# The first norm's rows kept feature set by feature set, for the experts' gather

## The chip, the cores and the metric

The program runs on one core of one Trainium2 chip. The metric is the device time of one execution in microseconds (us). A core has TensorE (PE, with its weight loads shown apart as PEld), VectorE (DVE), ScalarE (ACT), GpSimd (POOL) and SyncE (SP), whose queue issues the large transfers. All memory below is the on-chip memory of 128 partitions, unless HBM is named.

## The reference

Two layers over 256 tokens of 1024 features. A layer is a token mixer (three attention branches, gated, then an output projection), a norm, a mixture of experts, and a second norm. Cut to what matters here:

```python
for l in range(DEPTH):                                   # DEPTH = 2
    mix = token_mixer(x, ...)                            # ends with merged @ w_o
    x = layer_norm(alpha * x + mix, ln1_g[l], ln1_b[l])  # the first norm
    ffn = hier_moe(x, w_group, b_group, w_sub, b_sub, w1, w3, w2)
    x = layer_norm(alpha * x + ffn, ln2_g[l], ln2_b[l])

def hier_moe(t, ...):          # each token: the best of 4 groups, 2 of its 8 experts
    for e in range(N_EXPERTS):                           # 32 experts, hidden width 256
        h = jax.nn.silu(t @ w1[e]) * (t @ w3[e])
        y = y + combine[:, e:e + 1] * (h @ w2[e])
```

## The kernel before

**Tokens and experts.** The 256 tokens are two tiles of 128 (`t` = 0, 1), with tokens on partitions. An expert has 32 slots for tokens. Experts are worked on in quads of four, so a quad has 128 slots. The router finds a token's place in its experts; `dispatch` writes a 0/1 matrix "tokens by slots" from it.

**The gather.** For each of eight sets of 128 features, `gather_k` multiplies the transposed normed rows with the 0/1 matrix, so that a quad's 128 slots stand with features on partitions (`xg`). The stationary operand is `self.xn[:, t, k + i]`, 128 tokens by 128 features, and the moving operand is 128 slots of the 0/1 matrix. A product of f32 operands is two pairs of weight load and matmul. A quad takes 8 sets x 2 token tiles x 2 = 32 pairs; a layer has 8 quads. ScalarE then applies the norm's gain and bias out of PSUM (L1654). The first quad is gathered before the experts start; of each later quad, 16 pairs run ahead of the second product of the quad before and 16 behind it.

**Which features make a set.** Set k is the features f = 8q + k with q = 0..127, because a partition of the experts' weights holds eight consecutive features. `self.xn` is therefore a view of the row tile:

```python
self.xn = self.x.rearrange("p t (q k) -> p t k q", k=KD)   # KD = 8, set once per layer
```

A stationary tile of this view takes every eighth f32 of a row, 32 bytes apart. `ln1_xn` (steps `X0`, `X1`) writes the norm without gain and bias over `x` itself, in order. `ln1_out` reads `x` in order for the residual rows (with gain and bias, 512 features at a time) that start the second norm's sums.

**What sets the order.** Each engine runs its instructions in the order of the program text. From the output projection to the first experts that order is the list `END`: `... X0 X1 E s00 ... s16 N e0 e1 rk G3 pl pm d0 d1 cb g2 ct wt g0 g4 g6 st si`. `X` is the norm, `E` loads the table for the exponentials, `e` are the router's exponentials, `cb` its weights (DVE), `wt` the weighted 0/1 matrix (POOL, L1641), `g` gathers, and `st` transposes the weighted matrix (TensorE, L1663). Then `moe` goes from quad to quad: w1 product and w3 product (L1691), gather of half of the next quad, transposes (L1737), second product (L1771, behind the other half of the gather from the second quad on), and sums over slots (L1757) one quad later.

**Weights and slots.** All large tiles, temporaries and weights, share 24 slots of 8 KiB a partition (`Slots`). `Ring` issues the weights on SP's queue in order of use, each as soon as a dry pass over the program says that a slot can be spared until its use. A layer's experts have some 100 MB of weights, in transfers of 1 MB for most of them; the last quad's w3 and w2 come in pieces of 256 and 512 KB (L193).

Of the kernel before, what the change touches and what calls it, by code (L numbers as in the profile page):

```python
# [10 lines left out]
F32 = mybir.dt.float32  # L11
# [33 lines left out]
# Columns of the output projection, and of the last experts' second product: the last ones are few, as a norm waits for them.  # L45
# [5 lines left out]
# Splits of weights run so many pieces ahead of their products.  # L51
# [4 lines left out]
# The steps of the last layer's end.  # L56
# [5 lines left out]
# The piece by which a queue of attention steps is to be through, and the tensor work left for what lies between two steps.  # L62
# [53 lines left out]
class Slots:  # L116
    """8 KiB slots that the weight stream and the large temporaries share."""
# [23 lines left out]
    def part(self, name, n):  # L141
        """One of n parts of a slot."""
        for p in self.shared[n]:
            if p["free"]:
                return Part(self, n, p, p["free"].pop())
        p = {"tile": self.alloc([P, n, 2048 // n], F32, name), "free": set(range(1, n))}
        self.shared[n].append(p)
        return Part(self, n, p, 0)
# [17 lines left out]
class Ring:  # L166
    """Weights in the order of their use, each loaded as soon as a slot can be spared until then.

    `plan` is what a dry pass over the program has found: the slots that its temporaries hold after
    each change, and the change at which each weight tile is released."""  # L170
# [43 lines left out]
class Dry:  # L214
    """Stands for every object of the language in the dry pass."""
# [13 lines left out]
class Trunk:  # L229
# [35 lines left out]
    def evac(self, out, in_, n):  # L265
        """PSUM to SBUF on the engine of the two that has less to do."""
        if self.busy["act"] + 200 + 0.83 * n < self.busy["dve"] + 70 + 1.04 * n:
            self.note("act", n)
            self.nc.scalar.activation(out, in_, AF.Copy)
        else:  # L270
            self.note("dve", n)
            self.nc.vector.tensor_copy(out, in_)  # L272

    def split(self, hi, lo, src, n):
        """src = hi + lo exactly, each of 12 significant bits."""
        self.note("act", n)
        self.note("pool" if self.lo_pool else "dve", n)
        self.nc.scalar.activation(hi, src, AF.Copy)  # L278
        (self.nc.gpsimd if self.lo_pool else self.nc.vector).tensor_tensor(lo, src, hi.bitcast(F32), op=ALU.subtract)  # L279
# [7 lines left out]
    def warm(self, n, src):  # L287
        """Products that nobody reads: the tensor engine's clock falls to half when it has little to do."""
        ps = self.bank()
        for _ in range(n):  # L290
            self.nc.tensor.matmul(ps, src[:, 0:P], src[:, 0:512], start=True, stop=True)

# [105 lines left out]
    def load_small(self, l, home, o):  # L398
        """The layer's vectors, off the weights' queue; the router's weights behind the first o floats of a slot."""
# [19 lines left out]
    def small_T(self):  # L419
        """The vectors with their features on partitions; the router's weights with the gain of its input taken in."""  # L420
        nc = self.nc
        ps = self.bank()
        nc.tensor.transpose(ps[:, 0:P], self.v, self.ident)
        self.vec = self.t([P, 59], F32, "vecT", 1)
        nc.vector.tensor_copy(self.vec, ps[:, 0:59])
        self.hbg = self.t([P, 24], F32, "hbg", 1)
        nc.vector.tensor_scalar(self.hbg, self.vec[:, 3:27], 0.5, None, op0=ALU.mult)
        self.wg = self.t([P, KD, 36], F32, "wg", 1)
        w = self.wgb[:, :, 36:72]
        for j in range(2):  # L430
            g = self.vec[:, 27 + 8 * j:35 + 8 * j, None].broadcast_to([P, KD, 36])
            nc.gpsimd.tensor_tensor(self.wgb[:, :, 36 * j:36 * j + 36], w, g, op=ALU.mult)
        nc.gpsimd.tensor_copy(self.wg, self.wgb[:, :, 0:36])

    def small_rows(self):
        """Sums over the features: what a token's mean and the input's bias add to its logits."""
# [15 lines left out]
    def spread_gains(self, gb):  # L452
        """The first partition's rows to all."""
# [8 lines left out]
    def step(self, f, need=None, cost=0.45, key=None, after=()):  # L462
        """An attention step: what it needs marked, its tensor time, and steps that must lie some tensor time back."""
        self.q["steps"].append((f, need, cost, key, after))
# [17 lines left out]
    def run_fg(self, budget):  # L482
        """Attention steps worth so much tensor time, the most urgent first."""
# [7 lines left out]
    def run_fg_until(self, mark):  # L491
        """Everything of a branch that is left, other branches' steps where it would wait."""
# [6 lines left out]
    def rate(self, i):  # L499
        """Tensor time of attention steps that a piece must be joined by for all to be done when due."""  # L500
# [29 lines left out]
    def pieces(self, l):  # L530
        """The mixer's dense products in order: each is (key of its weights, last use, prepare, product)."""
# [67 lines left out]
        def gates(br, q):  # L599
            """Two 128-column tiles of a branch's gate."""  # L600
# [26 lines left out]
        def outp(br, w, kt, i, need):  # L627
            """A branch's output columns, gated and summed: 256 or 512 columns at a time."""
# [108 lines left out]
    def rope(self, v, t, nh, half, c, s):  # L737
        """Rotates the leading dims of [128, heads, dims] in place."""
# [13 lines left out]
    # -- branch A --  # L752
# [73 lines left out]
    # -- attention units: (block 0, four heads) or (block 1, two heads), 512 scores a row --  # L826
    def scores(self, us):
        """Score products, mask, maximum, exponentials of a unit, or of two on different rows of the array."""
# [38 lines left out]
    def probT(self, us):  # L867
        """Transposes of the 512 probability columns of one unit, or of two that share them."""
# [14 lines left out]
    def pv(self, ps, us, first, last):  # L883
        """Adds the outputs of two units, even heads and odd heads, each pair of heads in 128 columns."""
# [27 lines left out]
    def units_pipe(self, mk, oT, done, free, needs, first, joint):  # L912
        """Scores of a pair of units, then their transposes and outputs."""
# [63 lines left out]
    # -- branch C --  # L977
# [136 lines left out]
    # -- branch B --  # L1114
# [15 lines left out]
    def b_merge(self):  # L1130
        """Weights of the groups from their maxima and sums."""
# [167 lines left out]
    def mixer(self, l, acts):  # L1299
# [33 lines left out]
        self.xn = self.x.rearrange("p t (q k) -> p t k q", k=KD)  # L1333
# [19 lines left out]
    def table(self, func):  # L1353
        """Has the function's table loaded before it is waited for."""
# [3 lines left out]
    # -- first layer norm of a token tile, and the router's logits; x becomes twice alpha * x + the mixer's output  # L1358
    # (the products carry the gates' factor 2) --
# [30 lines left out]
    def grow(self):  # L1390
        """A slot more for the experts: half of it the rows of four, the rest two tiles of 512."""
# [7 lines left out]
    def ln1_rs(self, t):  # L1399
        """Mean, 1 / deviation, and the product's negative."""  # L1400
# [28 lines left out]
    def ln1_xn(self, t):  # L1429
        """The norm but for its gain and bias, in place."""  # L1430
        nc = self.nc
        mv = self.ln1[t][1]
        nmr = self.t([P, 1], F32, "nmr", 2)
        nc.gpsimd.tensor_tensor(nmr, mv[:, 3:4], mv[:, 2:3], op=ALU.mult)
        nc.scalar.activation(self.x[:, t], self.x[:, t], AF.Identity, bias=nmr, scale=mv[:, 2:3])

    def spread_row(self, j):
        """512 features of the first norm's gain (and then its bias), on all partitions."""
# [6 lines left out]
    def ln1_out(self, t, h):  # L1445
        """Half of a token tile's norm itself."""
        x = self.take()
        hs = slice(h * 512, (h + 1) * 512)
        g, b = self.gain1[h], self.gain1[2 + h]
        v = self.nc.vector  # L1450
        v.tensor_tensor(x, self.x[:, t, hs], g, op=ALU.mult)
# [3 lines left out]
    def residual(self, xs, h):  # L1455
        """Starts the token tiles' sums with their rows."""
# [4 lines left out]
    # -- second layer norm of a token tile --  # L1461
# [9 lines left out]
    def ln2_rs1(self, t):  # L1471
        """Mean, deviation, -1/2 of its square, of the sums that the chip holds over ALPHA."""
# [6 lines left out]
    def ln2_rs2(self, t):  # L1479
        """1 / deviation, and its product with the mean's negative."""  # L1480
# [17 lines left out]
    def next_T(self, t):  # L1498
        """The next layer's input, features on partitions."""
# [9 lines left out]
    def next_y(self, t, h):  # L1509
        """Half of it: gain and bias are a feature's own there."""  # L1510
# [17 lines left out]
    def ln2_out(self, t, acc, c, pool):  # L1528
        """A quarter of a token tile's rows of the last layer's output."""
# [13 lines left out]
    def route(self, l):  # L1543
        """The router, step by step: each token's best group, the first two of its experts, their weights, and its
        place among an expert's tokens. What a match replaces is the first of its value: among the first eight, a
        group, as the groups come before the experts."""
# [70 lines left out]
    def rows_of(self, e):  # L1617
        """The rows in the slots of four experts."""
        return self.xgs[e // Q % 2][:, 0:1024].rearrange("p (k c) -> p k c", k=KD)

    def dispatch(self, e0):
        """Tokens by slots of experts e0..e0+7."""
# [21 lines left out]
    def gather_k(self, pm, j, xg, k):  # L1644
        """Two times 128 features of the rows in the slots of four experts, gain and bias added."""
# [10 lines left out]
    def slots_T(self, e):  # L1656
        """Slots by tokens: the combine matrix of four experts and the weights of its slots."""
# [15 lines left out]
    def moe(self, l):  # L1673
# [9 lines left out]
        for e in range(0, NE, Q):  # L1683
# [111 lines left out]
            if e == NE - 2 * Q:  # L1795
                self.slots.free(self.x)
# [50 lines left out]
    def overflow(self, l, acc):  # L1847
        """Adds the outputs of the tokens past an expert's capacity."""
# [101 lines left out]
```

## Time and profile before

| | before |
|---|---|
| median of 3 runs, us | 1023.01 (1022.1 to 1024.78) |
| span of the profiled execution, us | 1022.9 |
| PE / PEld busy, us | 955.5 / 770.8 |
| DVE / ACT / POOL busy, us | 473.9 / 416.6 / 161.7 |
| read from HBM | 282.44 MB |
| mean granted clock of TensorE | 0.970 |

The profile is of one execution. The three runs are the device times of others. PE's busy time is a union over pipelined instructions, so it is not PE at its peak. The experts of the first layer run from some 300 to 505 us of the span, those of the second from some 808 to 1011 us.

### The profile page before, as it was taken

Reading aid. Unit: us, or ns where it says so; the run is one execution under the profiler, and the core shown is the slowest. Engines: PE = TensorE matmul, PEld = TensorE weight load, DVE = VectorE, ACT = ScalarE, POOL = GpSimd, SP = SyncE. Lnnn points to the kernel's source line nnn. Section 1 sums busy time; section 2 is a strip of 40 time slices with the busy share of each in tenths; the row PEclk is TensorE's granted clock in tenths of the full one; section 3 lists DMA queues with packets and bytes.
Section 4 is the critical chain, followed back from the end, with each engine's and each line's share of the span. In section 5 each row is a group of like instructions: output and inputs, shape, how many; then the busy total and the mean of one; then the engine's idle time right before and its main releaser. Section 6 shows DMA issues by size and latency. Waiting matters only on the chain.

```text
span 1022.9 us, 18674 instructions
## 1 busy us (share of the span) xinstructions
PE 955.5 (93%) x7584; PEld 770.8 (75%) x7591; DVE 473.9 (46%) x968; ACT 416.6 (41%) x911; POOL 161.7 (16%) x274
## 2 busy tenths in 40 slices
PE   8999999999999997879879999999999999977794
PEld 7888899899986774556469888998999867654462
DVE  5747776845642110111398586676455420101014
ACT  5545646644442221112345646665354422211131
POOL 4531210021100110000156071000311000000001
PEclk9999999999999998889989999999999999989898
DMA  9933261696969999999992134426968799999993
GB/s 330 328 103 124 79 210 42 220 340 216 365 241 380 417 400 419 418 417 375 376 340 68 64 124 128 162 90 224 330 232 321 288 379 420 419 419 417 419 370 121
DMA packets 100170, 284.76 MB, mean 278 GB/s; under 512 B 6324, under 2 KB 53808, under 8 KB 78576
## 3 DMA queue, kind: packets, MB, share of 16 engines
q1 hardware_dynamic: 99088, 283.12, 73.7%
q8 instruction: 62, 1.02, 0.4%
q0 software_dynamic: 992, 0.39, 0.2%
q14 instruction: 28, 0.23, 0.1%
HBM read 282.44 MB, written 1.05 MB: 277 GB/s over the span
## 4 chain that ended last, share of the span: by engine, by line
PE 68%; DMA 17%; issue 7%; POOL 3%; DVE 3%; SPq 1%; ACT 1%; POOLq 0%; DVEq 0%; ACTq 0%
DMA w<-in_w_dram 15%; PE bank L283 12%; PE bank L284 12%; PE bank L285 12%; PE bank L1650 7%; PE bank L1691 7%; PE bank L837 3%; PE bank L1771 3%; DMA w<-in_w_in_dram 2%; PE bank L891 2%; PE bank L878 2%; PE bank L1757 1%; PE bank L840 1%; PE bank L1459 1%; DVE xTl L279 1%
## 5 line engine op out<-in xcount | busy, mean ns | idle before, releaser
L279 DVE TENSOR_TENSOR ws<-w,ws 128x1024 fp32r<-128x1024 f32 (+2 forms) x154 | 184.7, 1208 | 133.1 <-ACT ws L278 124.2
L278 ACT ACTIVATE ws<-w 128x1024 fp32r<-128x1024 f32 (+2 forms) x158 | 159.0, 1023 | 35.5 <-PE bank L285 15.9
L1691 PE MATMUL bank<-w,xg 128*32 128x256 f32 x2048 | 139.6, 413 | 33.9 <-DMA w<-in_w_dram 24.4
L1691 PEld LDWEIGHTS bank<-w,xg 128*32 128x32 f32 x2048 | 70.2, 118 | 105.1 <-DMA w<-in_w_dram 30.5
L1650 PEld LDWEIGHTS bank<-xg,x 128*128 128x128 f32 x512 | 124.2, 334 | 3.0 <-issue 2.5
L1650 PE MATMUL bank<-xg,x 128*128 128x128 f32 x512 | 125.7, 399 | 0.0
L283 PE MATMUL bank<-ws,xTh 128*128 128x408 f32 (+3 forms) x320 | 116.6, 364 | 1.2 <-ACT xTh L278 1.2
L1654 ACT ACTIVATE xg<-bank,gpk 128x128 f32<-128x128 f32 x128 | 51.7, 454 | 159.3 <-PE bank L1650 159.3
L283 PE MATMUL bank<-xTh,ws 128*128 128x256 f32 x384 | 111.2, 290 | 0.0
L285 PE MATMUL bank<-ws,xTl 128*128 128x408 f32 (+3 forms) x320 | 110.6, 346 | 0.6 <-DVE xTl L279 0.6
L284 PE MATMUL bank<-ws,xTh 128*128 128x408 f32 (+3 forms) x320 | 110.3, 345 | 0.0
L284 PE MATMUL bank<-xTl,ws 128*128 128x256 f32 x384 | 108.6, 283 | 0.0
L285 PE MATMUL bank<-xTh,ws 128*128 128x256 f32 x384 | 108.5, 283 | 0.0
L1721 DVE SCALAR_TENSOR_TENSOR t<-t,cw,bank 128x256 f32<-128x256 f32 x16 | 10.8, 677 | 157.2 <-PE bank L1691 157.2
L283 PEld LDWEIGHTS bank<-xTh,ws 128*128 128x128 f32 x384 | 73.5, 191 | 1.8 <-issue 1.0
L284 PEld LDWEIGHTS bank<-xTl,ws 128*128 128x128 f32 x384 | 73.6, 192 | 0.2
L285 PEld LDWEIGHTS bank<-xTh,ws 128*128 128x128 f32 x384 | 73.5, 191 | 0.0
L283 PEld LDWEIGHTS bank<-ws,xTh 128*128 128x128 f32 x320 | 61.4, 192 | 8.1 <-ACT xTh L278 1.8
L853 ACT ACTIVATE p<-bank,nb 128x128 f32<-128x128 f32 (+1 forms) x92 | 37.3, 420 | 69.9 <-DVE nb L845 65.1
L285 PEld LDWEIGHTS bank<-ws,xTl 128*128 128x128 f32 x320 | 61.0, 191 | 5.9 <-DVE xTl L279 1.6
L284 PEld LDWEIGHTS bank<-ws,xTh 128*128 128x128 f32 x320 | 61.3, 192 | 3.4 <-DVE ws L279 0.3
L1771 PE MATMUL bank<-w,t 128*32 128x512 f32 (+1 forms) x544 | 59.1, 571 | 1.0 <-DVE t L272 1.0
(361 smaller groups left out, 1530.2 us busy)
## 6 DMA issues: line engine op xcount, KB each, us to landing
w<-in_w_dram SPq DMA_DIRECT2D x168, 1024.0 KB, 15.7
w<-in_w_gate_dram SPq DMA_DIRECT2D x24, 1024.0 KB, 5.3
w<-in_w_dram SPq DMA_DIRECT2D x80, 256.0 KB, 7.2
w<-in_w_in_dram SPq DMA_DIRECT2D x18, 1024.0 KB, 7.7
w<-in_w_in_dram SPq DMA_DIRECT2D x12, 816.0 KB, 12.8
w<-in_w_o_dram SPq DMA_DIRECT2D x8, 1024.0 KB, 8.8
w<-in_w_a_dram SPq DMA_DIRECT2D x4, 1024.0 KB, 6.1
w<-in_w_c_dram SPq DMA_DIRECT2D x4, 1024.0 KB, 5.1
```

The lines of the kernel that those rows point to most:

```text
L278: self.nc.scalar.activation(hi, src, AF.Copy)
L279: (self.nc.gpsimd if self.lo_pool else self.nc.vector).tensor_tensor(lo, src, hi.bitcast(F32), op=ALU.subtract)
L283: m(out, sh, mh, start=start, stop=False)
L284: m(out, sh, ml, start=False, stop=False)
L285: m(out, sl, mh, start=False, stop=stop)
L837: nc.tensor.matmul(b[:, j * w:(j + 1) * w], q[:, blk * P:(blk + 1) * P], k[:, 0:w], start=j == 0, stop=False)
L853: nc.scalar.activation(p[:, j], v[:, j], AF.Exp, bias=nb[:, j:j + 1], scale=u["scale"], accum_out=sm[:, j:j + 1])
L878: nc.tensor.transpose(ps[:, n * P:(n + 1) * P], p[:, j * P:(j + 1) * P], self.ident)
L1650: nc.tensor.matmul(ps[:, i * P:(i + 1) * P], self.xn[:, t, k + i], pm[:, t, j:j + Q].rearrange("p e c -> p (e c)"), start=t == 0, stop=t = ...
L1654: nc.scalar.activation(xg[:, k + i], ps[:, i * P:(i + 1) * P], AF.Identity, bias=b, scale=g)
L1691: nc.tensor.matmul(hp[i * CAP:(i + 1) * CAP, c * 256:(c + 1) * 256], xg[:, k, i * CAP:(i + 1) * CAP], w[i], start=k == 0, stop=k == KD - 1 ...
L1771: nc.tensor.matmul(yp[q * CAP:(q + 1) * CAP, :w], hT[:, j, q * CAP:(q + 1) * CAP], w2[q][:, j], start=j == 0, stop=j == 1, tile_position=( ...
```

## The change

`X0` takes one more slot, `xp`. `X0` and `X1` read `x` with a step of eight elements and write `xp` in order, set by set (k outer, q inner). The slot of `x` is freed after `X1`, and that of `xp` where `x` was freed before. The gather's stationary tiles are then 128 contiguous f32. `ln1_out` reads `xp` with a step of 128 elements between features that are neighbours in a row. The rest of the program text is the same but for comments.

```diff
@@ mixer @@
-        self.xn = self.x.rearrange("p t (q k) -> p t k q", k=KD)
+        self.xp = self.xn = None
@@ ln1_xn @@
+        if t == 0:
+            self.xp = self.slots.alloc([P, NT, D], F32, "xp")
+            self.xn = self.xp.rearrange("p t (k q) -> p t k q", k=KD)
         nmr = self.t([P, 1], F32, "nmr", 2)
         nc.gpsimd.tensor_tensor(nmr, mv[:, 3:4], mv[:, 2:3], op=ALU.mult)
-        nc.scalar.activation(self.x[:, t], self.x[:, t], AF.Identity, bias=nmr, scale=mv[:, 2:3])
+        nc.scalar.activation(self.xn[:, t], self.x[:, t].rearrange("p (q k) -> p k q", k=KD), AF.Identity, bias=nmr,
+                             scale=mv[:, 2:3])
+        if t == NT - 1:
+            self.slots.free(self.x)
@@ ln1_out @@
-        hs = slice(h * 512, (h + 1) * 512)
         g, b = self.gain1[h], self.gain1[2 + h]
         v = self.nc.vector
-        v.tensor_tensor(x, self.x[:, t, hs], g, op=ALU.mult)
+        xn = self.xn[:, t].rearrange("p k q -> p q k")[:, h * 64:(h + 1) * 64]
+        v.tensor_tensor(x.rearrange("p (q k) -> p q k", k=KD), xn, g.rearrange("p (q k) -> p q k", k=KD), op=ALU.mult)
         v.tensor_tensor(x, x, b, op=ALU.add)
@@ moe @@
             if e == NE - 2 * Q:
-                self.slots.free(self.x)
+                self.slots.free(self.xp)
```

The order of each engine's instructions stays as it was. One load of each layer gets other waits. On SP's queue at the end of the first layer's mixer, the weight loads before the change are (the words in brackets are what a load waits for; `DMAHW` is an earlier transfer of the same queue, of eight that may be under way):

```order
L195 DMA w_3265<-in_w_dram 128x2048 [waits DMAHW4_49]
L195 DMA w_3267<-in_w_dram 128x2048 [waits DMAHW5_49,PE_49]
L195 DMA w_3269<-in_w_dram 128x2048 [waits DMAHW6_49]
L195 DMA w_3415<-in_w_dram 128x2048 [waits DMAHW7_49,PE_49]
L195 DMA w_3425<-in_w_dram 128x2048 [waits DMAHW0_49,PE_49]
```

With the change the same place reads:

```order
L195 DMA w_3265<-in_w_dram 128x2048 [waits DMAHW4_49]
L195 DMA w_3267<-in_w_dram 128x2048 [waits DMAHW5_49,PE_49]
L195 DMA w_3316<-in_w_dram 128x2048 [waits DMAHW6_49,PE_49,Activation_49]
L195 DMA w_3416<-in_w_dram 128x2048 [waits DMAHW7_49,PE_49]
L195 DMA w_3426<-in_w_dram 128x2048 [waits DMAHW0_49,PE_49]
```

The third load has moved from the slot that `xp` now takes to the slot of `x`, and so waits for `X1` (Activation). Nothing else on this queue moved but for tile numbers. The second layer has the same in one load.

## Rows read from the trace of the kernel before

**Rows 1.** The page's costliest groups: the gather's weight loads and matmuls.

```profile
L1650 PEld LDWEIGHTS bank<-xg,x 128*128 128x128 f32 x512 | 124.2, 334 | 3.0 <-issue 2.5
L1650 PE MATMUL bank<-xg,x 128*128 128x128 f32 x512 | 125.7, 399 | 0.0
```

**Rows 2.** Chain that ended last, 286 to 301 us: start, us, what.

```profile
286.26 1.26 PE bank L1420 x12
...
291.56 0.99 PE bank L1442 x8
292.55 7.62 PE bank L1650 x32
```

**Rows 3.** Timeline, 289 to 320 us: start, us, engine, line; idle before.

```profile
288.09 2.36 ACT L1435 ACTIVATE x<-x,nmr,l1mv 128x1024 f32<-128x1024 f32 x2
...
293.20 0.31 ACT L1578 ACTIVATE es<-sub,neg 128x32 f32<-128x32 f32 x1
...
294.36 1.19 POOL L1641 TENSOR_TENSOR xg<-xg,comb 128x256 f32<-128x256 f32 x2 [3.52 <-DVE comb L1599]
...
301.45 18.25 SPq L195 DMA_DIRECT2D w<-in_w_dram  x10
...
304.05 0.69 DVE L1451 TENSOR_TENSOR xg<-x,bank 128x512 f32<-128x512 f32 x1 [2.21 <-PE bank L1691]
```

**Rows 4.** Groups by line and shape (busy, mean ns; idle): strided and plain DVE writes.

```profile
L720 DVE SCALAR_TENSOR_TENSOR t<-g,bank 128x256 f32<-128x256 f32 x32 | 12.8, 417 | 3.2 <-PE bank L285 3.0
...
L1721 DVE SCALAR_TENSOR_TENSOR t<-t,cw,bank 128x256 f32<-128x256 f32 x16 | 10.8, 677 | 157.2 <-PE bank L1691 157.2
```

**Rows 5.** Windows: length, busy by engine, PEclk, DMA share, GB/s.

```profile
295.00:300.00 5.00, 5.00 (x22) 5.00 (x22) 0.00 (x0) 1.92 (x5) 0.55 (x1) 1.00 0.27 107
305.00:345.00 40.00, 39.42 (x344) 26.64 (x340) 9.26 (x16) 9.92 (x26) 5.04 (x10) 1.00 0.99 393
380.00:385.00 5.00, 5.00 (x30) 4.13 (x33) 0.41 (x2) 2.53 (x8) 0.00 (x0) 1.00 1.01 418
390.00:395.00 5.00, 1.30 (x6) 0.38 (x10) 0.00 (x0) 0.00 (x0) 0.00 (x0) 0.61 1.01 419
455.00:460.00 5.00, 4.36 (x48) 2.15 (x52) 0.00 (x0) 0.00 (x0) 0.00 (x0) 0.56 1.01 419
805.00:810.00 5.00, 5.00 (x51) 4.07 (x54) 0.42 (x1) 2.86 (x7) 0.00 (x0) 1.00 0.01 2
810.00:860.00 50.00, 48.34 (x500) 31.57 (x496) 10.88 (x18) 11.89 (x31) 1.24 (x2) 1.00 0.98 392
```

**Rows 6.** Chain that ended last, 440 to 540 us.

```profile
442.20 13.40 DMA w<-in_w_dram
...
455.64 5.48 PE bank L1691 x58
...
461.58 3.66 PE bank L1691 x64
...
467.30 3.68 PE bank L1650 x16
...
471.21 3.81 PE bank L1650 x16
```

**Rows 7.** The last w2 load of each layer (issue, us to landing) and its product.

```profile
492.69 0.54 SPq L193 DMA_DIRECT2D w<-in_w_dram  x1
w<-in_w_dram SPq DMA_DIRECT2D x1, 256.0 KB, 6.0
502.69 1.07 PE L1771 MATMUL bank<-w,t 128*32 128x256 f32 x16
...
999.21 0.54 SPq L193 DMA_DIRECT2D w<-in_w_dram  x1
w<-in_w_dram SPq DMA_DIRECT2D x1, 256.0 KB, 5.9
1008.27 1.07 PE L1771 MATMUL bank<-w,t 128*32 128x256 f32 x16
```

## The prediction

> **What bounds the kernel now.** I read the page's groups first. The gather's 512 pairs of weight load and matmul keep PE busy for 125.7 us and PEld for 124.2 us [rows 1]. That is a large block, and the question is which of it the end waits for. The chain of waits answers that by stage.
>
> Ahead of the experts the chain runs through TensorE: 32 gather pairs take 7.62 us, 0.238 us a pair [rows 2]. The reader is to see the two neighbours of it there. In L1420, 12 instructions whose stationary tile is 128 contiguous f32 (36 columns moving) take 1.26 us, 0.105 us each. In L1442, 8 with 128 columns moving and one column repeated as stationary tile take 0.99 us, 0.124 us each. So neither 128 loaded nor 128 moving columns of f32 need 0.238 us. What the gather alone has is a stationary tile read with a step of 32 bytes.
>
> Then the stream of weights takes over. It has stopped while the first gather runs: 107 GB/s in 295 to 300 us and 2 GB/s in 805 to 810 us, against 418 when full [rows 5], because all slots hold weights and the first one comes free only with the first w1 product. SP issues again at 301.45 us [rows 3]. From there to 345 us it moves 393 GB/s, and in the second layer 392 from 810 to 860 us [rows 5]: nearly full, with some time lost where a load waits for a slot. From some 346 us on the chain is made of the stream, up to a load that lands at 442.20 + 13.40 = 455.6 us; TensorE follows at once, and from 455.64 us on the chain is TensorE again, with the last quad's two halves of a gather in it, 3.68 and 3.81 us [rows 6]. The last w2 load of the first layer lands at 492.69 + 6.0 = 498.7 us and is used at 502.69 us, 4.0 us later; in the second layer 999.21 + 5.9 = 1005.1 against 1008.27 us, 3.2 us later [rows 7].
>
> So a layer's experts are: a gather that holds up the stream, a stream that sets the pace, and a tail of TensorE with 3 to 4 us in hand. The six quads between are under the stream, and what their gathers save is mostly waited away.
>
> **The change, part by part.**
>
> The gather's pair. Its stationary tile becomes contiguous. No row has a contiguous f32 load together with 128 moving columns, so I bound it by 0.105 and 0.124 us and take the middle, 0.114 us. The first gather then takes 32 x 0.114 = 3.65 us in place of 7.62, and ends at 292.55 + 3.65 = 296.2 us, not at 300.17 (292.55 + 7.62): 4.0 us less. The two halves at a layer's end take 2 x 16 x 0.114 = 3.65 us for 3.68 + 3.81 = 7.49 us: 3.8 us less. [...]
>
> The norm's read. `X0` and `X1` now read `x` with the 32-byte step. They take 2.36 us together [rows 3]. No ScalarE row reads with a step. The lower bound is no cost. Two rows show a step's price elsewhere: the gather's pair, (0.238 - 0.114) us over 128 columns, 1.0 ns an element; and on DVE L1721, which writes its 256 results with a step, 677 ns against 417 for L720 of the same shape and kind, also 1.0 ns an element [rows 4]. I take 1.0 ns as the nearest, a read with this very step: 1024 x 1.0 = 1.0 us for each norm, 2.0 us for both; as an upper bound twice that. [...]
>
> What waits for the norm. Behind `X0` and `X1` in ScalarE's order stand the table load and the router's exponentials, the last of which ends at 293.20 + 0.31 = 293.5 us. DVE's L1599 waits for them, POOL's `wt` for that, and `wt` ends at 294.36 + 1.19 = 295.55 us [rows 3]; the transposes `st` stand behind the gather on TensorE and need it. Today `wt` is done 4.6 us before the gather. With 2.0 us added it ends at 297.6 us, behind the new end of the gather at 296.2. So the first w1 product comes 300.17 - 297.6 = 2.6 us earlier, and not 4.0. The gather's own start is covered: `X1` would end at 292.5, about when the 0/1 matrix lets the gather start today (292.5).
>
> The residual rows. Eight DVE multiplies (L1451, 0.69 us [rows 3]) read with a step of 512 bytes: from nothing up to 512 x 1.0 ns = 0.5 us each. They cost nothing, because DVE starts them when the w1 product frees a slot, and the next thing TensorE needs from DVE is L1721 behind the whole w3 product (3.66 us [rows 6]): four operations of 0.69 us, 2.8 us, fit, and 3.8 us would make L1721 some 0.2 us late at worst. Without that cover it would be 1 us a layer.
>
> The extra slot. One load of a layer waits for `X1` and starts some 3 to 6 us later than now. The stream is idle afterwards until the first w1 product [rows 5], so it loses nothing; the loads behind it wait for that product anyway. `xp` takes a slot that was free for a load, so `X0` has no new wait.
>
> The stream. It restarts 2.6 us earlier in each layer. Up to 345 us it falls short of 418 GB/s by 25/418 x 40 = 2.4 us, and in the second layer by 26/418 x 50 = 3.1 us [rows 5]. Part of that is loads that wait for a slot that the first quads' products free; these come earlier by the gathers between (2 us per half). I count two thirds, 1.6 + 2.0 = 3.6 us; the bounds are 0 and 5.5.
>
> The tails. In the first layer, TensorE has 3.8 us less to do after its last wait, and the last load 4.0 us in hand: all 3.8 count. In the second it has only 3.2 us in hand, then the stream's end binds: 3.2 count.
>
> Sum: 2 x 2.6 + 3.6 + 3.8 + 3.2 = 15.8 us. The profiled execution's span is 1022.9 us and the median of the runs 1023.01, so 0.1 us apart; the forecast is 1007 us. With the norm's step free, 2 x 1.4 us more, and the whole shortfall, 1.9 more, it is 1002; with the norm's step at twice the price (4 us less) and no shortfall gained (3.6 less) 1015.
>
> **The rivals.**
>
> *The stream takes it all but the restart.* If the last loads come later against TensorE than I think (the small pieces of the last quad move more slowly, and they are limited by eight under way), then only the two restarts count: 5.2 to 8.0 us, 1015 to 1018. For it: the stream is full in between. Against it: 4.0 and 3.2 us in hand [rows 7].
>
> *The step is not what makes the pair long.* Then the gather stays as it is and the norm's bill hides behind it (4.6 us of room): 1023, no change. For it: no row of before has a contiguous f32 load of 128 with 128 moving. Against it: L1420 and L1442 between them show each half.
>
> [...]
>
> **How the numbers follow.** Forecast as summed 0.75, the stream takes it 0.15, no change 0.06, slower 0.04. A measurement of this kernel tells about 0.3%, 3 us, from no change. The first two cases are faster (0.90, of which I leave 0.02 to a gain too small to tell), so faster 0.88, within 0.3% 0.08, slower 0.04. The range takes the forecast's bounds, 1002 to 1015, and the nearer part of the second case, up to 1016.
>
> **What would show it.** Right: L1650's group of before (a later line now) falls from 125.7 to some 60 us of PE, with a load well under 334 ns; the norm takes 3.4 to 4.5 us for both tiles; the first w1 product starts 2 to 4 us after a gather that ends near 296 us; SP's restart is at 297.5 to 299 us; the waits for weights grow in the middle quads. Wrong: a gather's pair still near 0.23 us; a norm of 6 us or more; a wait for w2 of more than 1 us ahead of the last products; a granted clock below 1 for more than 10 us behind the last wait.

## The result, and the profile after

| | after | before, on the same chip |
|---|---|---|
| median of 4 runs, us | 1011.19 (1009.72 to 1014.45) | 1023.89 (1022.1 to 1025.21) |
| ratio after / before | 0.9866, 95% interval 0.9834 to 0.9898 | |
| span of the profiled execution, us | 1008.0 (its run: 1009.72) | 1022.9 |
| PE / PEld busy, us | 903.2 / 707.6 | 955.5 / 770.8 |

The changed kernel is 1.3% faster: 12.7 us by the medians, 14.9 us by the two spans. TensorE is busy for 52.3 us less. The page's costliest groups, with busy time, mean ns of one, and idle time ahead of them, show both halves of this:

```profile
L1697 PE MATMUL bank<-w,xg 128*32 128x256 f32 x2048 | 150.0, 428 | 68.3 <-DMA w<-in_w_dram 59.1
...
L1656 PE MATMUL bank<-xg,xp 128*128 128x128 f32 x512 | 63.0, 276 | 2.0 <-ACT xg L1660 2.0
L1656 PEld LDWEIGHTS bank<-xg,xp 128*128 128x128 f32 x512 | 60.6, 192 | 5.9 <-issue 2.5
```

The gather (L1656 now) answers to [rows 1]: a weight load takes 192 ns for 334, and the group 63.0 us for 125.7. The w1 and w3 products (L1697) now wait 59.1 us for weights. The same group in the kernel before says how much of that is new:

```profile
L1691 PE MATMUL bank<-w,xg 128*32 128x256 f32 x2048 | 139.6, 413 | 33.9 <-DMA w<-in_w_dram 24.4
```

So of 62.7 us saved in the gather, 34.7 us turned into longer waits for the stream. Another 10.4 us went into the w1 and w3 products themselves, 150.0 us for 139.6: with more waits between them the mean granted clock fell from 0.970 to 0.953.

The timeline of the changed kernel ahead of the first experts (start, us, engine, line; idle before) answers to [rows 3]:

```profile
287.94 4.37 ACT L1438 ACTIVATE xp<-x,nmr,l1mv 128x1024 f32<-128x1024 f32 x2
...
292.24 2.85 PE L1656 MATMUL bank<-xg,xp 128*128 128x128 f32 x24
...
295.06 0.31 ACT L1584 ACTIVATE es<-sub,neg 128x32 f32<-128x32 f32 x1
295.27 2.87 ACT L1660 ACTIVATE xg<-bank,gpk 128x128 f32<-128x128 f32 x8
...
296.11 1.16 PE L1656 MATMUL bank<-xg,xp 128*128 128x128 f32 x8 [1.02 <-ACT xg L1660]
296.21 1.19 POOL L1647 TENSOR_TENSOR xg<-xg,comb 128x256 f32<-128x256 f32 x2 [5.52 <-DVE comb L1605]
...
297.10 0.68 PE L1669 MATMUL bank<-cst,xg 128*128 128x128 f32 x2
...
297.71 3.66 PE L1697 MATMUL bank<-w,xg 128*32 128x256 f32 x64
```

The two norms take 4.37 us where they took 2.36. The router's exponentials end at 295.37 us, 1.9 us later than before, and POOL's weighted matrix at 297.40. The first w1 product starts behind it, at 297.71. The same stretch of the chain that ended last runs through these engines and no longer through the gather:

```profile
295.78 0.43 DVE comb L1605 x2
...
296.79 0.62 POOL xg L1647
...
297.45 0.33 PE bank L1669
297.78 3.35 PE bank L1697 x57
```

Before, all of 292.55 to 300.17 us was the gather [rows 2]. On SP's queue the next weights go out at 298.84 us, against 301.45 [rows 3]. Windows of the changed kernel (length, busy by engine, PEclk, DMA share, GB/s) answer to [rows 5]:

```profile
295.00:300.00 5.00, 3.90 (x55) 2.60 (x58) 1.69 (x9) 4.97 (x15) 1.19 (x2) 1.00 0.33 129
305.00:345.00 40.00, 38.84 (x437) 23.44 (x430) 9.57 (x15) 10.89 (x28) 5.03 (x10) 1.00 1.00 408
...
810.00:860.00 50.00, 42.45 (x476) 25.11 (x472) 9.66 (x16) 14.07 (x36) 1.23 (x2) 0.98 1.01 418
```

The stream still stops ahead of the experts, but then moves 408 and 418 GB/s where it moved 393 and 392. At the first layer's end, the timeline shows the last long wait and the last quad's gather:

```profile
451.54 5.30 PE L1697 MATMUL bank<-w,xg 128*32 128x256 f32 x58 [1.44 <-DMA w<-in_w_dram]
...
462.87 1.95 PE L1656 MATMUL bank<-xg,xp 128*128 128x128 f32 x16
...
464.87 1.95 PE L1656 MATMUL bank<-xg,xp 128*128 128x128 f32 x16
```

The last wait ends at 451.54 us, 4.1 us earlier than the 455.64 of [rows 6], and each gather half takes 1.95 us. (From the third quad on, both halves run ahead of the second product of the quad before; only the second quad's gather has that product between its halves.) The second layer has the same wait, before (first fence) and after:

```profile
961.05 5.35 PE L1691 MATMUL bank<-w,xg 128*32 128x256 f32 x58 [1.49 <-DMA w<-in_w_dram]
```

```profile
950.45 5.02 PE L1697 MATMUL bank<-w,xg 128*32 128x256 f32 x58 [1.44 <-DMA w<-in_w_dram]
```

### The profile page after: what moved, and what is told of

Same layout as the page of the kernel before. It is cut to its first block, busy times and chain, and to the rows that moved or that the text cites. A ratio compares the mean times of both kernels' runs of the same rounds, so it can differ in the third digit from the quotient of the medians.

```text
span 1008.0 us, 18682 instructions
## 1 busy us (share of the span) xinstructions
PE 903.2 (90%) x7590; PEld 707.6 (70%) x7591; DVE 476.8 (47%) x968; ACT 419.4 (42%) x911; POOL 161.3 (16%) x274
## 3 DMA queue, kind: packets, MB, share of 16 engines
q8 instruction: 62, 1.02, 0.4%
## 4 chain that ended last, share of the span: by engine, by line
PE 60%; DMA 22%; issue 7%; POOL 3%; DVE 3%; ACT 2%; SPq 1%; POOLq 0%; DVEq 0%; ACTq 0%
DMA w<-in_w_dram 20%; PE bank L283 13%; PE bank L284 12%; PE bank L285 12%; PE bank L1697 6%; PE bank L837 3%; PE bank L1777 2%; PE bank L891 2%; PE bank L878 2%; PE bank L1656 2%; DMA w<-in_w_in_dram 1%; PE bank L840 1%; PE bank L1763 1%; ACT xp L1438 1%; PE bank L1465 1%
## 5 line engine op out<-in xcount | busy, mean ns | idle before, releaser
L1697 PE MATMUL bank<-w,xg 128*32 128x256 f32 x2048 | 150.0, 428 | 68.3 <-DMA w<-in_w_dram 59.1
L1697 PEld LDWEIGHTS bank<-w,xg 128*32 128x32 f32 x2048 | 71.9, 122 | 148.1 <-DMA w<-in_w_dram 70.1
L278 ACT ACTIVATE ws<-w 128x1024 fp32r<-128x1024 f32 (+2 forms) x158 | 158.9, 1023 | 35.7 <-PE bank L285 15.9
L1727 DVE SCALAR_TENSOR_TENSOR t<-t,cw,bank 128x256 f32<-128x256 f32 x16 | 10.8, 677 | 200.5 <-PE bank L1697 200.5
L1660 ACT ACTIVATE xg<-bank,gpk 128x128 f32<-128x128 f32 x128 | 50.9, 453 | 95.3 <-PE bank L1656 92.7
L1722 ACT ACTIVATE t<-bank 128x256 f32<-128x256 f32 x16 | 6.2, 384 | 147.3 <-PE bank L1697 147.3
L1656 PE MATMUL bank<-xg,xp 128*128 128x128 f32 x512 | 63.0, 276 | 2.0 <-ACT xg L1660 2.0
L1656 PEld LDWEIGHTS bank<-xg,xp 128*128 128x128 f32 x512 | 60.6, 192 | 5.9 <-issue 2.5
```

The source lines that it names most:

```text
L1656: nc.tensor.matmul(ps[:, i * P:(i + 1) * P], self.xn[:, t, k + i], pm[:, t, j:j + Q].rearrange("p e c -> p (e c)"), start=t == 0, stop=t = ...
L1660: nc.scalar.activation(xg[:, k + i], ps[:, i * P:(i + 1) * P], AF.Identity, bias=b, scale=g)
L1697: nc.tensor.matmul(hp[i * CAP:(i + 1) * CAP, c * 256:(c + 1) * 256], xg[:, k, i * CAP:(i + 1) * CAP], w[i], start=k == 0, stop=k == KD - 1 ...
```

## The experiments

The theory is the prediction's: the step of 32 bytes made the gather's pair long, and the time comes back at three places, the restart of the stream (first quad), the stream's shortfall (middle quads), and the tail behind the last wait (last quad). The rivals: the stream takes all but one of these; or the norm's bill, or a lower clock, decides. The kernels ran in three groups: k0_after and e1 to e3, e4 to e7, and k1_after with e8 to e10. Those of a group share a chip and its runs of the kernel before (medians 1024.83, 1024.08 and 1024.55 us). A ratio goes by the means of all runs but the first, profiled one, so it need not be that of the medians. A kernel's ratio is known to some 0.002, about 2 us.

### The changed kernel again

k0_after and k1_after are the changed kernel without an edit.

> The changed kernel again, as the measure for the others of this call. Both theories: its span near 1008 us, about 15 us under the kernel before.

> The changed kernel once more, beside the three below on one chip. Both theories: 1009 to 1013 us, first w1 product 5.5 us behind the gather's start in both layers.

Measured: k0_after 1011.09 us, ratio 0.9865 (0.9844 to 0.9886), and k1_after 1008.68 us, ratio 0.9858 (0.9837 to 0.9880). The medians of one kernel differ by 2.4 us between the groups, the ratios by 0.0007. So kernels of two groups are compared by ratios below.

### The old view for some quads only

In these three the norm writes the new tile as in the changed kernel, and the gather of some quads reads it with a step of eight. Those quads get other features than the reference's; the work and its shape are the same. The edit, with the condition of each:

```diff
@@ ln1_xn @@
             self.xn = self.xp.rearrange("p t (k q) -> p t k q", k=KD)
+            self.xs = self.xp.rearrange("p t (q k) -> p t k q", k=KD)
@@ gather_k @@
+        xn = self.xs if 0 < e < NE - Q else self.xn      # e1_mid; e2_first: e == 0; e3_last: e == NE - Q
-                nc.tensor.matmul(ps[:, i * P:(i + 1) * P], self.xn[:, t, k + i], ...
+                nc.tensor.matmul(ps[:, i * P:(i + 1) * P], xn[:, t, k + i], ...
```

> Stationary tiles with the 32-byte step for the six middle quads of each layer alone (192 of 256 pairs of a layer); these take wrong features, so only the time counts. Theory that the stream of weights sets the pace between the first and the last quad: at most 3 us longer than the changed kernel (the part of the stream's shortfall that the first of these gathers had closed, 1.7 and 1.2 us). Rival that every quad's gather counts alike: six eighths of the 15 us are lost, 11 us.

> The 32-byte step for the first quad's gather of each layer alone (wrong features there). Theory that this gather holds up the restart of the stream: 2.4 to 2.6 us a layer, 5 us longer than the changed kernel, with SP's restart near 301.4 us in the first layer. Rival that every quad counts alike: one eighth of 15, 1.9 us.

> The 32-byte step for the last quad's gather of each layer alone (wrong features there). Theory that this gather lies on the tail behind the last wait for weights: 3.3 us in the first layer and 3.7 in the second, 7 us longer than the changed kernel, and no wait for the last w2 load any more. Rival that every quad counts alike: 1.9 us.

| | median, us | over k0_after | ratio to before |
|---|---|---|---|
| e1_mid | 1015.78 | 4.7 | 0.9917 (0.9899 to 0.9936) |
| e2_first | 1015.4 | 4.3 | 0.9906 (0.9886 to 0.9927) |
| e3_last | 1016.82 | 5.7 | 0.9927 (0.9908 to 0.9946) |

By the medians each place is worth about a third: 4.7 + 4.3 + 5.7 = 14.7 us, and before less k0_after is 1024.83 - 1011.09 = 13.7. By the traces below it is some 2, 4.9 and 7.7 us. The intervals of e1_mid and e3_last lie clear of k0_after's; that of e2_first touches it. That every quad counts alike (11, 1.9 and 1.9 us) falls by e1_mid and e3_last, and in e2_first by the trace. The middle quads are the cheapest for what they do. They hold six of the eight gathers, and the page of e1_mid has the gather at 110.3 us:

```profile
L1658 PE MATMUL bank<-xg,xp 128*128 128x128 f32 x512 | 110.3, 369 | 2.0 <-ACT xg L1662 2.0
```

The w1 and w3 products, with their waits for weights, in e1_mid and then in k0_after:

```profile
L1699 PE MATMUL bank<-w,xg 128*32 128x256 f32 x2048 | 139.3, 414 | 33.2 <-DMA w<-in_w_dram 23.7
```

```profile
L1697 PE MATMUL bank<-w,xg 128*32 128x256 f32 x2048 | 149.2, 425 | 68.1 <-DMA w<-in_w_dram 58.9
```

110.3 us against 63.0 is 47 us more of gather. 35 us of it is taken out of waits, and 10 us out of the products, which are shorter as the mean granted clock is 0.969 for 0.948. What is left, some 2 us, shows in the window of 810 to 860 us, of e1_mid and then of k0_after:

```profile
810.00:860.00 50.00, 48.84 (x435) 33.97 (x434) 8.89 (x14) 12.72 (x33) 1.24 (x2) 1.00 0.99 401
```

```profile
810.00:860.00 50.00, 43.01 (x476) 25.26 (x472) 9.35 (x16) 14.05 (x36) 1.23 (x2) 0.95 1.01 418
```

With long gathers in the middle the stream moves 401 GB/s there in place of 418: the slots come free later, as SP's queue waits 29 us in this window for TensorE's products, for 17 us in k0_after. By this window that is at most 17/418 x 50 = 2.0 us of stream. From the first w1 product to the end of the last long wait it is 1.1 us in the first layer (155.25 us for 154.19) and 0.8 us in the second (153.07 for 152.29). The two profiled spans are 2.0 us apart (1009.8 and 1007.8), less than the medians say; the profiled execution of e1_mid was the shortest of its six. The size of this part is therefore known only as 2 to 5 us: the expected "at most 3 us" holds in the traces and not by the medians.

In e2_first the gather ends last again. Its timeline has no wait in front of the first w1 product:

```profile
293.42 7.79 PE L1658 MATMUL bank<-xg,xp 128*128 128x128 f32 x32
...
301.35 3.01 PE L1699 MATMUL bank<-w,xg 128*32 128x256 f32 x52
```

The product starts 7.93 us behind the gather's start, against 297.71 - 292.24 = 5.47 us with the change: 2.46 us a layer, 4.9 for both, and 4.3 by the medians. In e3_last the last quad's halves are long again:

```profile
462.60 3.85 PE L1658 MATMUL bank<-xg,xp 128*128 128x128 f32 x16
466.50 3.98 PE L1658 MATMUL bank<-xg,xp 128*128 128x128 f32 x16
```

That is 3.93 us more in a layer (3.85 + 3.98 - 2 x 1.95), 7.9 for both; 5.7 are left by the medians. In the traces, the time from the end of the last long wait to the layer's last product (L1765 here, L1763 in k0_after) is 49.7 and 49.6 us for 45.6 and 45.9, so 7.7 us for both layers. No product waits for the last w2 load any more, as expected.

### What the norm's bill costs

e4_norm_in_order writes the norm to the new tile without reordering, so that both sides of the norm are contiguous. The gather then reads other features than the reference's.

```diff
-        nc.scalar.activation(self.xn[:, t], self.x[:, t].rearrange("p (q k) -> p k q", k=KD), AF.Identity, bias=nmr,
-                             scale=mv[:, 2:3])
+        nc.scalar.activation(self.xp[:, t], self.x[:, t], AF.Identity, bias=nmr, scale=mv[:, 2:3])
```

> The norm reads and writes its rows in order, as before the change, and everything else is as changed, so the gather and the residual rows take features in a wrong order and only the time counts. Theory that the norm's step costs 1.0 us a tile and that the first w1 product waits for it through the router's exponentials: the first w1 product comes 1.2 to 1.4 us earlier in each layer than in the changed kernel, 2.5 us in all. Rival that the norm's longer read lies beside other work: no earlier.

Measured: 1009.09 us, ratio 0.9830 (0.9804 to 0.9856). The timeline shows what the bill holds up:

```profile
288.11 2.36 ACT L1438 ACTIVATE xp<-x,nmr,l1mv 128x1024 f32<-128x1024 f32 x2
...
292.40 3.74 PE L1655 MATMUL bank<-xg,xp 128*128 128x128 f32 x32
...
294.37 1.19 POOL L1646 TENSOR_TENSOR xg<-xg,comb 128x256 f32<-128x256 f32 x2 [3.52 <-DVE comb L1604]
...
296.29 1.07 PE L1696 MATMUL bank<-w,xg 128*32 128x256 f32 x16
```

The norm is back at 2.36 us, the gather runs through in 3.74 us, and the first w1 product starts 3.89 us behind the gather's start: 1.6 us a layer earlier than in the changed kernel. The last long wait of the first layer ends at 450.21 us, where it ends at 451.5 to 451.9 in the three traces of the changed kernel. The ratio is 0.003 lower than those of k0_after and k1_after, as 3.2 us would make it, but the intervals overlap. So the bill's place and size are shown by the trace; its effect on the whole time is likely and not shown clear of the spread.

e5_write and e9_write (the same kernel) put the step on the write of the norm and read in order.

```diff
+        nc.scalar.activation(self.xn[:, t].rearrange("p k q -> p q k"), self.x[:, t].rearrange("p (q k) -> p q k", k=KD), AF.Identity,
+                             bias=nmr, scale=mv[:, 2:3])
```

> The norm reads x in order and writes xp with a step (512 bytes between neighbours), the same values in the same places as in the changed kernel. If a step costs ScalarE only where it reads: 1.23 us a tile, and the first w1 product 1.2 to 1.4 us earlier in each layer. If a write with a step costs as much as on DVE (1.0 ns an element): 2.2 us a tile, and no change.

> The norm with the step on its write (2.13 us each) instead of its read (2.23 us), repeated: its first run was 3.6 us under the changed kernel's by medians of two calls, while its trace has the first w1 product only 0.3 us earlier per layer. If the trace says what it is worth, it is 0.3 to 1.0 us under k1 and its interval cannot be told from k1's; rival: the step on the write really is worth 3 us or more (something later reads or waits better), then 3 us or more under k1 again.

Its norms, by line (count, ns min/median/max, first and last start, shape):

```profile
L1438 ACT ACTIVATE xp<-x,nmr,l1mv x4: 2101/2126/2150, 287.9 to 792.0; 128x1024 f32<-128x1024 f32 x4
```

2126 ns, hardly less than 2232 with the step on the read. The first run gave 1007.5 us (0.9836, 0.9819 to 0.9854), 3.6 us under k0_after; beside k1_after the second gave 1008.67 us (0.9856, 0.9838 to 0.9874) for 1008.68. There is no gain to be seen: the two ratios of this one kernel differ by 0.0020, which is the spread of a ratio. Of the two theories of e5_write the second holds (2.2 us a tile, and no change): a step on ScalarE's write costs nearly what it costs on its read. The rival of e9_write, 3 us or more, falls.

### Which step costs

In e6_steps, which ran once, the gather of the third, fourth and fifth quad reads with steps of 2, 4 and 8 f32, and the norms of the two token tiles read with steps of 8 and 4 in the first layer, and 2 and 1 in the second. Features are mixed up by it.

```diff
+STEP = {8: 2, 12: 4, 16: 8}                                  # first expert of a quad: step
@@ gather_k @@
+            return self.xp[:, t].rearrange("p (q s) -> p s q", s=step)[:, k % step, 0:P]     # stationary tile of these quads
@@ ln1_xn @@
+        n = ((8, 4), (2, 1))[self.layer][t]
+        nc.scalar.activation(self.xp[:, t].rearrange("p (k q) -> p k q", k=n), self.x[:, t].rearrange("p (q k) -> p k q", k=n), AF.Identity,
+                             bias=nmr, scale=mv[:, 2:3])
```

> One look for durations, with wrong features: the gathers of quads 2, 3 and 4 take stationary tiles with a step of 2, 4 and 8 f32 (8, 16 and 32 bytes), the others contiguous ones; and the norms of the four row tiles (two a layer) read with a step of 8, 4, 2 and 1 f32. [...] Rival that any step pays: the step of 2 as long as that of 8.

Measured: 1009.93 us. The timeline has a half gather (16 pairs) with step 2, then 4, then 8, then a contiguous one, and with it ScalarE's two norms of each layer:

```profile
328.60 2.05 PE L1665 MATMUL bank<-xg,xp 128*128 128x128 f32 x16
...
347.86 3.90 PE L1665 MATMUL bank<-xg,xp 128*128 128x128 f32 x16
...
374.70 3.98 PE L1665 MATMUL bank<-xg,xp 128*128 128x128 f32 x16
...
404.31 1.95 PE L1665 MATMUL bank<-xg,xp 128*128 128x128 f32 x16
```

```profile
287.78 4.35 ACT L1441 ACTIVATE xp<-x,nmr,l1mv 128x1024 f32<-128x1024 f32 x2
...
790.01 2.44 ACT L1441 ACTIVATE xp<-x,nmr,l1mv 128x1024 f32<-128x1024 f32 x2
```

Both engines have one edge, between 2 and 4; a step of 3 was not run. Step 2 costs 0.1 us in 16 pairs (the same half takes 1.95 us in k0_after; the second quad's contiguous halves take 2.05 in every trace) and 0.08 us in two norms (2.44 for 2.36). So the rival that any step pays falls. Step 4 costs nearly as much as step 8: 3.90 and 3.98 us for 1.95, and 4.35 us for the norms with steps 8 and 4, as two with step 8 take 4.37. Why the edge lies there, no run shows.

### The wait that was left

With the change TensorE waits for the router's weights ahead of the first w1 product. e7_order and e10_order (the same kernel) issue the router's exponentials behind the first half of the gather's evictions, and the transposes behind the first w1 product instead of ahead of it. e8_order_write adds the write of e5_write.

```diff
-       "... N e0 e1 rk G3 pl pm d0 d1 cb g2 ct wt g0 g4 g6 st si")
+       "... N rk G3 pl pm d0 d1 g2 g0 e0 e1 g4 g6 cb ct wt si")
@@ moe @@
-        pm, nxt = self.disp, self.nxt
+        pm, nxt = self.disp, None
...
                     nc.scalar.activation(si, hp[:, 0:256], AF.Silu)
+                    if e == 0:
+                        nxt = self.slots_T(0)
```

> The changed kernel with another order: the first two of the first gather's four groups ahead of the router's exponentials on ScalarE, and the transposes of the weighted matrix behind the first w1 product. The reference's output. Theory that the first w1 product waits for the exponentials and for a free bank of the gather: it starts at the gather's end, 1.8 us earlier in each layer, 3.6 us in all. Rival that the stream's restart is not what the layer waits for: no change.

> The order with the router's exponentials and the transposes behind the first gather, repeated beside k1. The trace of its first run has the first w1 product 3.7 us behind the gather's start in place of 5.5, so 1.8 us a layer: 3 to 4 us under k1 if the stream's restart sets the end; 0 to 1 us if the stream takes it back.

> Both edits, the order of e10 and the write of e9. If the norm's bill counts only through the wait of the first w1 product for the router's weights, the order has removed that wait and this is within 1 us of e10 (the gather's start may come up to 0.2 us earlier). Rival, the write itself is worth 3 us: 3 us under e10, near 1004 us.

The timeline of e7_order, from the gather on:

```profile
292.19 3.74 PE L1656 MATMUL bank<-xg,xp 128*128 128x128 f32 x32
...
295.86 3.66 PE L1697 MATMUL bank<-w,xg 128*32 128x256 f32 x64
```

The first w1 product follows the gather at once, 3.67 us behind its start for 5.47: 1.8 us a layer. Measured: e7_order 1007.12 us, ratio 0.9826 (0.9799 to 0.9852); e10_order 1008.17, 0.9838 (0.9820 to 0.9856); e8_order_write 1005.95, 0.9835 (0.9814 to 0.9856), beside k1_after's 1008.68 and 0.9858 (0.9837 to 0.9880). All three lie 0.002 to 0.004 under the changed kernel, near the 3.6 us that the trace gives, and each interval overlaps its. In their traces the last long wait of the first layer ends at 448.7 to 449.9 us, in the three of the changed kernel at 451.5 to 451.9. The order is probably worth 2 to 4 us; that it beats the change is not shown beyond the spread. The write adds nothing that can be told from e10_order.

## Why the prediction was right

The time came out at 1011.2 us, in the range of 1002 to 1016, 4 us above the forecast. Step by step:

**The pair.** Forecast 0.114 us, counted from start to start. A gather's half now takes 464.65 - 462.87 = 1.78 us from its start to that of the next instruction, 0.111 a pair; the timeline's 1.95 us (2.05 in the second quad) also has the rest of its last product. The step was the cause: e1_mid to e3_last bring the long pair back with nothing but the view, and e6_steps does it inside one kernel. The rival "the step is not what makes the pair long" falls. The prediction bounded the pair by L1420 and L1442; a nearer row stood on the page of the kernel before, weight loads of 128 neighbouring elements at 191 ns, as the gather's now take 192:

```profile
L283 PEld LDWEIGHTS bank<-xTh,ws 128*128 128x128 f32 x384 | 73.5, 191 | 1.8 <-issue 1.0
```

**The norm's bill.** Forecast 1.0 us for each; measured 2.23 for 1.23 us. The price of a step taken from TensorE's rows held on ScalarE.

**The wait ahead of the first w1 product.** Forecast 2.6 us earlier in each layer, since the weighted matrix would end at 297.6 us; it ended at 297.40, and the product came 300.32 - 297.71 = 2.6 us earlier in the first layer. Not foreseen: the gather's last 8 pairs stop for 1.02 us. They need a PSUM bank whose eviction on ScalarE (L1660) stands behind the late exponentials. It cost nothing beside the wait for POOL, and both go away in e4 and e7.

**The residual rows.** Forecast up to 0.5 us each; L1457 takes 1.07 us for 0.69. They stayed hidden as argued: L1727 in the first quad waits for the w3 product and not for them.

```profile
305.75 0.67 DVE L1727 SCALAR_TENSOR_TENSOR t<-t,cw,bank 128x256 f32<-128x256 f32 x1 [0.79 <-PE bank L1697]
```

**The extra slot.** One load waits for `X1`, as forecast, and holds SP for 4.7 us in the stretch in which nothing else could have been issued:

```profile
SPq L195 <- ACT xp L1438: 4.7, 1, 4.7
```

**The stream and the tails.** The last long wait ends 455.64 - 451.54 = 4.1 us earlier in the first layer; less the restart's 2.6 the stream regained 1.5 us (forecast 1.6). In the second layer the wait ends 961.05 - 950.45 = 10.6 us earlier. The spans are 14.9 us apart; the first layer's end is 7.6 us earlier by the records (505.34 and 497.78 us), so its tail gave 7.6 - 4.1 = 3.5 (forecast 3.8), as its last w2 product now takes 1.55 us for 1.07 [rows 7], with a wait for its load in the middle:

```profile
495.17 0.57 PEld L1777 LDWEIGHTS bank<-w,t 128*32 128x32 f32 x10 [0.35 <-DMA w<-in_w_dram]
```

The second layer gave 14.9 - 7.6 = 7.3 us. Its first w1 product starts at 798.00 us for 808.04, 10.0 earlier, so 2.4 came at the restart; 10.6 - 10.0 = 0.6 by the stream (forecast 2.0), and 14.9 - 10.6 = 4.3 in the tail (forecast 3.2). Together 2.6 + 1.5 + 3.5 + 2.4 + 0.6 + 4.3 = 14.9 us, against 15.8: the tails gave 7.8 where 7.0 were counted, the stream 2.1 where 3.6 were. That these two errors have opposite signs is luck, and that two thirds of the shortfall come back was a choice that no row gave.

What caps a tail is what the prediction said, the stream's end, and in both layers of this trace it now binds. The last loads are paced by their own queue: SP's waits in the second layer's tail before the change (us, times, longest), and then the last w2 load with it:

```profile
SPq L193 <- DMA w<-in_w_dram: 23.9, 21, 3.2
```

```profile
987.47 0.54 SPq L193 DMA_DIRECT2D w<-in_w_dram  x1
w<-in_w_dram SPq DMA_DIRECT2D x1, 256.0 KB, 5.9
```

It lands at 987.47 + 5.9 = 993.4 us, when its product has already begun (993.14). That is 42.9 us behind the last long wait, where it was 1005.1 - 961.05 = 44.1 before [rows 7]. So the 4.3 us are, but for rounding, the 3.2 in hand and 1.2 by which these loads were quicker. In the first layer they were 0.6 slower (495.1 - 451.54 = 43.6 us for 43.0), which makes 3.4 of the 4.0 in hand. In three traces of the changed kernel this time scatters from 42.3 to 43.6 us, so the mis-sized term, the cap, could not have been known to better than 1 us.

**From span to run.** The forecast took a run as 0.1 us above the span. In the runs it is 1.7 (1009.72 and 1008.0). The pair of numbers before was of different executions. That is 1.6 us of the 4.2 by which the forecast was low, 0.9 are the sum's, and 1.5 is how far the median of four runs lies above the profiled one; the rest is rounding. The gain by medians was 12.7 us here, and 13.7 and 15.9 us in the groups of k0_after and k1_after.

**The rivals.** "The stream takes all but the restart" gave 1015 to 1018; e3_last, without the tails' gain, has 1016.8, so the tails are what tells this case from the rival. "Slower", at 0.04, did not come. The granted clock fell, 0.953 for 0.970 as a mean, but not where it would have counted: the w1 and w3 products of all quads take 10.4 us more, between waits for the stream, while in the tail the last quad's take 13.7 us, as they did before (496.04 - 482.36 us). Right behind the last waits the clock was below 1 for less than the 10 us that the prediction gave as a sign against it: in the windows of the changed kernel it is 0.51 in 451.54 to 455.00 us and 1.00 in 455 to 470, and in the second layer 0.54 in 950.45 to 953.50 and 1.00 in 953.50 to 969.

## What to carry to other kernels

Ask of every large group with a step in its operand whether a contiguous copy can be had where the data is written once and read often: here two norms paid 2 us a layer and 32 gather pairs a quad got 4 back, eight times. But count the gain by place: of 62.7 us saved on TensorE 15 came through, two thirds of it (more by the traces) from the first and the last of a layer's eight gathers; most of the rest was waited away behind the stream or went into products at a lower granted clock (0.953 for 0.970 as a mean). And a tail gives only what it has in hand against the last loads. When the producer gets slower, look at what stands behind it in its engine's order, as that becomes the next wait; moving those instructions is the next edit.

## What the runs showed of the hardware

**The step's edge.** In e6_steps, 16 gather pairs with a stationary f32 tile of step 2 took 2.05 us, where contiguous ones took 1.95; with step 4 they took 3.90 and with step 8 3.98. ScalarE's two norms took 2.44 us reading with steps 2 and 1, where they took 2.36 in order, and 4.35 with steps 8 and 4, where two with step 8 took 4.37. On ScalarE a step on the write cost about the same as on the read here, 2126 (e5_write) and 2232 ns (the changed kernel) for 1230 in order. On VectorE, L1457, which reads with a step of 512 bytes, took 1.07 us, where the same multiply in order took 0.69.

**The clock in the tail.** The w1 and w3 products of a layer's last quad took 13.7 us in one layer of k0_after and 12.0 in the other. The windows over just these products (length, busy by engine, PEclk, DMA share, GB/s):

```profile
474.47:488.15 13.68, 13.68 (x147) 6.45 (x147) 0.00 (x0) 2.47 (x4) 0.00 (x0) 0.88 0.98 345
972.70:984.69 11.99, 11.99 (x147) 5.78 (x147) 0.00 (x0) 2.47 (x4) 0.00 (x0) 1.00 0.98 340
```

TensorE is busy throughout in both; the mean granted clock is 0.88 in the one and 1.00 in the other. What TensorE did before is the same in both, the last quad's gather, the second product of the quad before and eight small products (L458). What decides it was not tried. But the 1.7 us do not reach the layer's end. From the last long wait to the last product the two layers take 45.6 and 45.9 us, as the one with the faster products then waits for its w2 loads:

```profile
987.33 0.16 PEld L1777 LDWEIGHTS bank<-w,t 128*32 128x32 f32 x8 [0.70 <-DMA w<-in_w_dram]
```

What reaches it is a low clock for longer. The whole tail of the first layer, in k0_after and then in e4_norm_in_order:

```profile
451.85:497.47 45.62, 44.54 (x423) 22.70 (x424) 8.46 (x17) 9.59 (x21) 0.00 (x0) 0.93 1.01 376
```

```profile
450.21:498.44 48.23, 46.78 (x420) 23.21 (x424) 8.46 (x17) 9.59 (x21) 0.00 (x0) 0.87 1.02 378
```

Of the 24 layers traced with a contiguous last gather, 16 have a tail of 45.0 to 46.2 us and eight one of 47.9 to 48.3, both layers of e4_norm_in_order and of e10_order among them, and no layer in the three traces of the changed kernel. In the eight the mean granted clock over the 10 us behind the last wait is 0.73 to 0.76, in the others 0.77 to 0.87. This is some 2.5 us a layer that comes and goes without an edit to the tail. It is probably much of why runs of one kernel spread over some 4 us and why 2 us could not be settled here; the executions without a trace cannot tell.
